# Values of all heads as seven products of quarters, with sums formed beside the state space

## The chip, the cores and the metric

The program runs on one core of one Trainium2 chip. The metric is the device time of one execution in microseconds. A profile of one execution gives, for every engine, what it did and what it waited for: TensorE (PE, with its weight loads as PEld), VectorE (DVE), ScalarE (ACT), GpSimd (POOL) and SyncE (SP). Here SP issues the program's DMAs, in one queue and in order.

## What is computed

A trunk of two layers over 1024 tokens of width 1024, in float32. Layer 0 projects the normalised input once and feeds a diagonal state space with a GLU beside a retention of 8 heads (4 pairs in the kernel). Layer 1 is a convolution module. The change concerns the retention's values `v` and the work in front of them.

```python
proj = h @ w_in                       # h = rmsnorm(x) * g, (1024, 1024)
u_s5, g_s5, q, k, v, g_ret = jnp.split(proj, cuts, axis=-1)   # v: (1024, 1024)
...
qc, kc = rope(q) * DK ** -0.5, rope(k)          # in chunks of 64 tokens
scores = jnp.einsum('bnihd,bnjhd->bnhij', qc, kc) * intra
intra_out = jnp.einsum('bnhij,bnjhe->bnihe', scores, vc)
kv = jnp.einsum('bnjhd,jh,bnjhe->bnhde', kc, k_dec, vc)
_, s_prev = lax.scan(state_step, zeros, kv)     # s <- chunk_decay * s + kv
cross = jnp.einsum('bnihd,ih,bnhde->bnihe', qc, q_dec, s_prev)
out = layernorm_per_head(intra_out + cross)
y_ret = out * jax.nn.silu(g_ret)
```

## The kernel before

**Matmuls.** Each float32 operand is split into a high part (cast to float32r) and a low part (the rest). A product is three matmuls: high x high, high x low, low x high. A matmul takes 128 rows of the inner dimension against 128 columns of the stationary and up to 512 of the moving operand; a full projection of one 128-column block and one half of the tokens (512) is 8 row blocks (`KB`) x 3.

**Scaling.** x is kept transposed (channels in partitions) and multiplied by the norm's gain `g`, but not by the reciprocal root of each token's mean square. This factor is applied when a result leaves PSUM: `R` along the free dimension for transposed results, `Rtok` per partition for results that have tokens in partitions, as the values do. `self.xs[h][kb]` holds the pair (high, low) of half h of the tokens and row block kb, in two rings of 16 buffers (`opA`, tags A0 and A1). They are held until the last projection has read them; then y, the state space's output, takes their place for the GLU.

**Weights.** `plan` lists all weight tiles (512 KB) in the order of their use. `wnext` issues the loads up to two tiles ahead; `wload` casts the high part on ScalarE and forms the low part on GpSimd or VectorE. There are three buffers of each kind.

**Order.** The program is built in an order of priorities, and the scheduler puts each engine's instructions into a fixed order with a model of the times. `issue_after(x)` keeps what it encloses behind the instruction x. `at(p)` sets a priority. On the chip every engine then keeps its own order and waits on semaphores. A pool's buffers are taken in rotation by tag; a pool that takes the place of a closed one waits for the old tiles.

**Stages.**

1. `layer0_front`: x is loaded and split; u projections (blocks 0 to 7); then 16 gate blocks (8 to 23), beside which the state space of 8 blocks runs: tables on GpSimd (`s5_tables`, one call per block, the last at gate block 19), the scan on VectorE (`s5_states`), outputs on TensorE (`s5_out`). At gate blocks 16 to 23 `weight_sums` forms sums of the output weights' quarters on VectorE and stores them: 4 loads, 4 operations and 4 stores of 256 KB for one half tile.
2. `retention`: for each of four pairs of heads `ret_proj` (k, then q, each 48 matmuls of 512 columns; evacuation on VectorE; the rotation by four DMAs that exchange rows, two products on GpSimd and an addition on VectorE), the values, two `y_pass` (gelu of two blocks of the state space's output, in pairs 1 to 3 behind the last rsqrt of the pair before), and `ret_heads`: transposed k (ktp), k-v products (kv) and their running state on VectorE, scores (sp), masked on VectorE, outputs (ro), the norm on VectorE and ScalarE, transposition back (rt) and the gate. There is one buffer each for the turned k and q, and two for their raw forms.
   - The values of pairs 0 and 1 come together in pair 0 (`ret_values_wide`): 2 token halves x 4 token blocks x 8 row blocks x 3 terms, 512 columns.
   - The values of pairs 2 and 3 come in those pairs (`ret_values`): 8 token blocks x 8 row blocks x 3 terms, 256 columns each.
   - Pair 2's k projection is asked for ahead of pair 1's heads (`ahead`).
   - In pair 0 `weight_low` forms 16 half tiles of low parts of the convolution's weights and stores them; the other 16 are formed in the GLU.
3. `layer0_back_and_layer1`: GLU, output projection (by seven products of quarters already), the convolution module, the last norm.

PSUM has 8 banks: 3 for projections (`mm`) and 5 for the rest (`aux`).

Of the kernel before, what the change touches and what calls it, by code (L numbers as in the profile page):

```python
# [11 lines left out]
F32 = mybir.dt.float32  # L12
# [7 lines left out]
P = 128  # L20
# [18 lines left out]
           [(i, nb) for i in (6, 7) for nb in range(4)] + [(4, nb) for nb in range(4)])  # L39


V_NG0, V_NG1, V_FG, V_GLUB, V_CB, V_LNG, V_LNB = range(7)


# [11 lines left out]
class Trunk:  # L56
# [22 lines left out]
    def plan(self):  # L79

        A = self.A
        seq = [(A["w_ab"][nb], f"u{nb}") for nb in range(8)]
        seq += [(A["w_ab"][nb], f"g{nb}") for nb in range(8, 24)]
        for p in range(4):
            seq += [(A["w_ab"][28 + p], f"k{p}"), (A["w_ab"][24 + p], f"q{p}")]

            if p == 0:
                seq += [(A["w_v"][j], f"v{p}_{h}_{j}") for h in range(2) for j in range(4)]
            elif p > 1:
                seq += [(A["w_v"][2 * p + i], f"v{p}_{i}") for i in range(2)]  # L90
# [17 lines left out]
        self.ws_d = {}  # L108
        self.wnames, self.lo_d = {n for _, n in seq}, {}

    def wnext(self, name, ahead=2):
# [8 lines left out]
    def wload(self, src, name):  # L120


        if src is None:
# [43 lines left out]
    def wload_sums(self, name):  # L167

        i, nb = int(name[1]), int(name[3])
        src = self.A["w_out"][{1: 0, 2: 8, 4: 12}[i] + nb] if i in (1, 2, 4) else self.ws_d[i, nb]  # L170
        return self.wload_split(self.wload_f32(src, name), name, self.nc.vector)

    def weight_low(self, pool, k, tags, bufs):

# [111 lines left out]
    def layer0_front(self, st):  # L286
# [134 lines left out]
        u_block(3)  # L421
        u_block(4)
        early.close()
        self.s5 = self.pool("s5w", 1, stack=st)
        sums = self.pool("sums", 1, stack=st)
        for nb in range(5, 8):
            u_block(nb)
        self.s5_tab, self.s5_back, self.s5_last = {}, {}, None
# [1 line left out]
        for nb in range(8, 24):  # L430
# [5 lines left out]
                self.s5_out(B - 1)  # L436
            if nb % 2 and B < 7:
                self.s5_tables(B + 1)
            if nb >= 16:
                with self.tc.issue_after(self.gate_evac.ins):  # L440
# [428 lines left out]

    def retention(self, st):  # L870
        nc, A = self.nc, self.A
        rp = self.rp = self.pool("ret", 1, stack=st)
        early = ExitStack()
        rq = self.rq = self.pool("retq", 1, stack=early, side="right")
        self.rk = rq.tile([P, 2, T], F32, name="ropek")
        nc.sync.dma_start(self.rk[:], A["rope_k"])
        self.mask = rp.tile([P, NH, P], F32, name="retmask")
        nc.sync.dma_start(self.mask[:], A["ret_mask"])
        self.kdec = rp.tile([P, NH, 64], F32, name="kdec")
        nc.sync.dma_start(self.kdec[:], A["ret_kdec"])  # L880
        self.g128 = rp.tile([P, 4], F32, name="g128")
        nc.sync.dma_start(self.g128[:], A["ret_g128"])
        self.reps = rp.tile([P, NH], F32, name="reteps")
        nc.sync.dma_start(self.reps[:], A["ret_eps"])
        ahead = None
        for pair in range(4):
            cur = list(ahead or self.ret_proj(pair))[-1]

            ahead = pair == 1 and self.ret_proj(pair + 1)
            if ahead:  # L890
                next(ahead)
            if pair == 0:
                V = self.ret_values_wide()
            elif pair > 1:
                V = self.ret_values(pair)
            with ExitStack() as held:
                if pair:
                    held.enter_context(self.tc.issue_after(self.last_rs.ins))
                for cb in (2 * pair, 2 * pair + 1):
                    self.y_pass(rq, cb)  # L900

            def turned():
                if pair == 3:
                    early.close()
                    self.lp = self.pool("l1", side="right")
            for k in range(LOWS if pair == 0 else 0):
                self.weight_low(rq, k, (("wa", "wb"), ("wc", "wd")), 2)
            self.ret_heads(pair, *cur, V, turned)

    def ret_proj(self, pair):  # L910
        nc, A, rp = self.nc, self.A, self.rp
        raws = {}

        def project(nm):
# [36 lines left out]
            qadds = ()  # L951
        yield krot, qrot, qadds

    def ret_values(self, pair):

        nc = self.nc
        wv = [self.wnext(f"v{pair}_{i}") for i in range(2)]
        vt = self.rp.tile([P, 8, 256], F32, name=f"v_{pair}", tag="v", bufs=2)
        for b in range(8):
            ps = self.bank(f"mm_v{pair}_{b}", aux=False)  # L960
            h, o = b // 4, (b % 4) * P
            for kb in range(KB):
                xh, xl = self.xs[h][kb]
                i, k4 = kb // 4, kb % 4
                wh = wv[i][0][:].rearrange("p (k a) n -> p k (a n)", a=2)[:, k4, :]
                wl = wv[i][1][:].rearrange("p (k a) n -> p k (a n)", a=2)[:, k4, :]
                nc.tensor.matmul(ps[:, :256], xh[:, o:o + P], wh, start=kb == 0, stop=False)
                nc.tensor.matmul(ps[:, :256], xh[:, o:o + P], wl, start=False, stop=False)
                nc.tensor.matmul(ps[:, :256], xl[:, o:o + P], wh, start=False, stop=kb == KB - 1)
            nc.scalar.mul(vt[:, b, :], ps[:, :256], self.Rtok[:, b:b + 1])  # L970
        return lambda p, b, hh: vt[:, b, hh * P:(hh + 1) * P]

    def ret_values_wide(self):

        nc = self.nc
        res = []
        for h in range(2):
            vt = self.rp.tile([P, 4, HALF], F32, name=f"v_0_{h}", tag="v", bufs=2)
            pss = [self.bank(f"mm_v0_{h}_{b}") for b in range(4)]
            for j in range(4):  # L980
                wh, wl = (t[:].rearrange("p (k a) n -> p k (a n)", a=4) for t in self.wnext(f"v0_{h}_{j}"))
                for b in range(4):
                    o = slice(b * P, (b + 1) * P)
                    for k in range(2):
                        kb = 2 * j + k
                        xh, xl = self.xs[h][kb]
                        nc.tensor.matmul(pss[b][:], xh[:, o], wh[:, k, :], start=kb == 0, stop=False)
                        nc.tensor.matmul(pss[b][:], xh[:, o], wl[:, k, :], start=False, stop=False)
                        nc.tensor.matmul(pss[b][:], xl[:, o], wh[:, k, :], start=False, stop=kb == KB - 1)
            for b in range(4):  # L990
                nc.scalar.mul(vt[:, b, :], pss[b][:], self.Rtok[:, 4 * h + b:4 * h + b + 1])
            res.append(vt)
        return lambda p, b, hh: res[b // 4][:, b % 4, (2 * p + hh) * P:(2 * p + hh + 1) * P]

    def ret_heads(self, pair, K, Q, qadds, V, turned):
        nc, rp = self.nc, self.rp
# [620 lines left out]
def layout(inp):  # L1617
# [10 lines left out]
    wv = w[:, 3072:4096].reshape(2, 4, P, 4, 256)  # L1628
    A["w_v"] = wv.transpose(3, 0, 2, 1, 4).reshape(8, P, KB, P)
    A["w_v"][:4] = w[:, 3072:3584].reshape(4, 2, P, HALF).transpose(0, 2, 1, 3).reshape(4, P, KB, P)  # L1630
# [49 lines left out]
```

## Time and profile before

| what | us |
|---|---|
| median of 3 runs | 1197.28 (1195.81 to 1198.75) |
| the profiled execution | 1195.29 |
| its span, first to last instruction | 1193.5 |
| TensorE busy | 1177.1 |
| VectorE, GpSimd, ScalarE busy | 870.5, 679.5, 533.8 |
| k and q of pair 0 on TensorE | 337.1 to 359.0 |
| values of pairs 0 and 1 | 359.0 to 402.5 |
| heads of pair 0, with k and q of pair 1 among them | 402.5 to 437.1 |
| heads of pair 1 begin, pair 2, pair 3 | 448.0, 494.6, 552.3 |

The mean granted clock of TensorE was 0.998 of full speed. How to read the views: a row of the stretches gives from:to in us, its length, then busy us and count for each engine, the granted clock, the mean busy share of the 16 DMA engines and GB/s. A row of the chain or of the timeline begins with start and duration. A row of a tile gives durations in ns (least/median/most) and the first and last start. "Busy" of pipelined matmuls says that some matmul was under way, not that the engine was at its peak.

### The profile page before, as it was taken

The page shows a single profiled execution, that of the slowest core. Times are in us where ns is not written, and L with a number is a line of the kernel's source. Part 1 is how long each engine was busy: PE and PEld are TensorE (multiplying, and loading weights), DVE is VectorE, ACT ScalarE, POOL GpSimd, SP SyncE. Part 2 cuts the span into 40 slices and gives each one's busy share as a digit, 9 for nine tenths or more (in the row PEclk, how much of TensorE's full clock was granted, in tenths as well). Part 3 has the DMA queues.
Part 4 walks back from the last instruction along what each step waited for, and adds up shares of the span by engine and source line. Part 5 has one row for each costly group of instructions (what it writes and reads, how often), then busy time and mean ns, then how long its engine had stood idle before and what let it go on. Part 6 is the DMA issues. An engine that isn't in the chain of part 4 may idle for free.

```text
span 1193.5 us, 17692 instructions
## 1 busy us (share of the span) xinstructions
PE 1177.1 (99%) x6390; PEld 987.1 (83%) x6390; DVE 870.5 (73%) x1455; ACT 533.8 (45%) x805; POOL 679.5 (57%) x481
## 2 busy tenths in 40 slices
PE   9999999999999999999899999999999999999997
PEld 7888888888888888989788888878887887888887
DVE  7875655699836358366876888379999999999643
ACT  7212233332334322235445535367756578444662
POOL 2059988888426345242443034338895678987642
PEclk9999999999999999999999999999999999999999
DMA  9353333388889463556897467866448653356873
GB/s 338 107 181 102 124 124 131 122 281 286 268 299 337 175 183 102 176 157 227 312 327 247 147 222 266 292 228 205 163 150 296 233 176 115 134 187 239 268 255 135
DMA packets 119097, 248.13 MB, mean 208 GB/s; under 512 B 11489, under 2 KB 40417, under 8 KB 118881
## 3 DMA queue, kind: packets, MB, share of 16 engines
q1 hardware_dynamic: 119008, 247.00, 61.0%
q8 instruction: 50, 0.82, 0.3%
q14 instruction: 39, 0.31, 0.1%
HBM read 179.39 MB, written 63.37 MB: 203 GB/s over the span
## 4 chain that ended last, share of the span: by engine, by line
PE 93%; DVE 3%; POOL 1%; DMA 1%; issue 1%; ACT 0%; SPq 0%; DVEq 0%; POOLq 0%; ACTq 0%
PE mm_g L227 7%; PE mm_g L226 7%; PE mm_g L225 7%; PE mm_w L225 4%; PE mm_w L226 4%; PE mm_w L227 4%; PE mm_oc L225 2%; PE mm_oc L226 2%; PE mm_oc L227 2%; PE mm_u L227 2%; PE mm_u L226 2%; PE mm_u L225 2%; PE mm_glu L227 2%; PE mm_glu L225 2%; PE mm_glu L226 2%; PE mm_b L226 2%
## 5 line engine op out<-in xcount | busy, mean ns | idle before, releaser
L1368 DVE SCALAR_TENSOR_TENSOR cv<-u,convw,cv 128x512 f32<-128x512 f32 x358 | 245.3, 749 | 5.7 <-ACT cv L1354 3.9
L1348 POOL TENSOR_TENSOR tp<-tp,tp 128x512 f32<-128x512 f32 x104 | 138.7, 1335 | 33.6 <-ACT tp L1347 27.8
L227 PE MATMUL mm_g<-xh,wl_g 128*128 128x512 f32 x256 | 100.8, 394 | 0.0
L226 PE MATMUL mm_g<-xl,wh_g 128*128 128x512 f32 x256 | 100.6, 393 | 0.0
L225 PE MATMUL mm_g<-xh,wh_g 128*128 128x512 f32 x256 | 100.4, 392 | 0.0
L1347 ACT ACTIVATE tp<-u,convw 128x512 f32<-128x512 f32 x104 | 69.3, 713 | 9.2 <-POOL tp L1348 9.0
L226 PEld LDWEIGHTS mm_g<-xl,wh_g 128*128 128x128 f32 x256 | 48.1, 188 | 11.3 <-issue 1.6
L227 PEld LDWEIGHTS mm_g<-xh,wl_g 128*128 128x128 f32 x256 | 48.1, 188 | 10.5
L225 PEld LDWEIGHTS mm_g<-xh,wh_g 128*128 128x128 f32 x256 | 48.1, 188 | 9.6
L225 PE MATMUL mm_oc<-zh,wh_woc 128*128 128x512 f32 (+1 forms) x152 | 54.5, 362 | 0.0
L227 PE MATMUL mm_oc<-zh,wl_woc 128*128 128x512 f32 (+1 forms) x152 | 54.5, 359 | 0.0
L226 PE MATMUL mm_oc<-zl,wh_woc 128*128 128x512 f32 (+1 forms) x152 | 54.2, 356 | 0.0
L1159 POOL TENSOR_TENSOR yg<-yg,yn 128x512 f32<-128x512 f32 x16 | 24.1, 1507 | 50.4 <-DMA yg<-gs_d 27.3
L226 PE MATMUL mm_u<-xl,wh_u 128*128 128x512 f32 x128 | 50.1, 391 | 1.0 <-DVE xl L339 0.9
L227 PE MATMUL mm_g<-h1h,wl_cg 128*128 128x512 f32 x128 | 50.0, 390 | 1.1 <-POOL wl_cg L217 1.1
L226 PE MATMUL mm_b<-h1l,wh_cb 128*128 128x512 f32 x128 | 50.5, 394 | 0.4 <-DVE h1l L1285 0.4
L225 PE MATMUL mm_glu<-yh,wh_glu 128*128 128x512 f32 x128 | 50.4, 394 | 0.0
L163 ACT CAST wh_p<-wf_p 128x1024 fp32r<-128x1024 f32 x28 | 29.5, 1053 | 46.7 <-PE mm_w L226 37.8
L225 PE MATMUL mm_g<-h1h,wh_cg 128*128 128x512 f32 x128 | 50.3, 393 | 0.0
L225 PE MATMUL mm_b<-h1h,wh_cb 128*128 128x512 f32 x128 | 49.9, 390 | 0.4 <-ACT h1h L1284 0.4
L227 PE MATMUL mm_a<-h1h,wl_ca 128*128 128x512 f32 x128 | 50.3, 393 | 0.0
L227 PE MATMUL mm_glu<-yh,wl_glu 128*128 128x512 f32 x128 | 50.2, 393 | 0.0
(790 smaller groups left out, 3664.8 us busy)
## 6 DMA issues: line engine op xcount, KB each, us to landing
wf_g<-w_ab SPq DMA_DIRECT2D x16, 512.0 KB, 5.2
a<-w_out SPq DMA_DIRECT2D x32, 256.0 KB, 5.3
ws<-a SPq DMA_DIRECT2D x32, 256.0 KB, 4.2
lf<-w_c SPq DMA_DIRECT2D x32, 256.0 KB, 5.7
wf_p<-ws SPq DMA_DIRECT2D x16, 512.0 KB, 3.8
wf_cb<-w_c SPq DMA_DIRECT2D x16, 512.0 KB, 4.7
wf_ca<-w_c SPq DMA_DIRECT2D x16, 512.0 KB, 4.8
wl_cb<-lo_cb SPq DMA_DIRECT2D x16, 512.0 KB, 3.4
```

Of the source, the lines that this page charges most:

```text
L163: self.nc.scalar.copy(wh[:].rearrange(fl), wf[:])
L225: nc.tensor.matmul(ps, wh[:, kb, :], xh, start=start, stop=False)
L226: nc.tensor.matmul(ps, wh[:, kb, :], xl, start=False, stop=False)
L227: self.last_mm = nc.tensor.matmul(ps, wl[:, kb, :], xh, start=False, stop=stop)
L1159: gp.tensor_tensor(yg[:], yg[:], yn[:], op=ALU.mult)
L1347: nc.scalar.mul(sk[:], u[:, k:k + HALF], cw[:, nb, k:k + 1])
L1348: gp.tensor_tensor(s0[:], s0[:], sk[:], op=ALU.add)
L1368: v.scalar_tensor_tensor(dst[:], *tap, accs_[i][:], op0=ALU.mult, op1=ALU.add)
```

## The change

The values of all four pairs are formed ahead of pair 0's heads. x (tokens x channels) and the weights of v (channels x columns) are cut into quarters of 512 x 512. Seven products of sums of quarters, each 512 x 512 x 512, replace the eight plain products; the four quarters of v are sums of the seven results, formed on VectorE as the products leave PSUM, and then scaled by `Rtok` on ScalarE.

- `input_sums` (new; at gate blocks 9, 11, 13, 15) forms four sums of x's quarters, times the gain, on ScalarE and VectorE and stores them in DRAM.
- `value_sums` (new; four half tiles at gate block 21, behind the last state-space table) forms four sums of the weights' quarters on GpSimd and stores them.
- `ret_values` (new form) runs the products in the order 1, 2, 6, 7, 3, 4, 5. Products 1, 2 and 3 use x's operands as they stand; for 6, 7, 4 and 5 `fetch` loads a stored sum of x and splits it into high and low part. Weights come as 14 tiles (`V1_0` to `V5_1`); products 6, 7, 3 and 5 take the stored sums.
- The values of pairs 2 and 3 are no longer formed in those pairs, and pair 2's k projection is no longer asked for ahead of pair 1's heads.
- `weight_low`'s 16 half tiles move from pair 0 to pairs 1 and 2, eight each, behind the masked scores of the pair before. `y_pass` of pair 0 and the load of `kdec` come after the values, since their pools are opened there. Pools are placed anew.

```diff
+V_ORDER = (1, 2, 6, 7, 3, 4, 5)
...
             if p == 0:
-                seq += [(A["w_v"][j], f"v{p}_{h}_{j}") for h in range(2) for j in range(4)]
-            elif p > 1:
-                seq += [(A["w_v"][2 * p + i], f"v{p}_{i}") for i in range(2)]
+                seq += [(None, f"V{i}_{j}") for i in V_ORDER for j in range(2)]
...
+    def wload_value(self, name):
+        i, j = int(name[1]), int(name[3])
+        src = self.A["w_v"][{1: 0, 2: 2, 4: 6}[i] + j] if i in (1, 2, 4) else self.vs_d[i, j]
+        return self.wload_split(self.wload_f32(src, name), name, self.nc.vector if i in (1, 2, 6) or j else self.nc.gpsimd)
+
+    def value_sums(self, pool, k):
+        j, c = k // 2, slice(k % 2 * HALF, (k % 2 + 1) * HALF)
+        e, a = self.nc.gpsimd, []
+        for q, (r, tag) in enumerate(((0, "wa"), (4, "wb"), (6, "wc"), (2, "wd"))):
+            a.append(pool.tile([P, HALF], F32, name=f"va{q}_{k}", tag=tag, bufs=2))
+            self.nc.sync.dma_start(a[q][:], self.A["w_v"][r + j].rearrange("p k n -> p (k n)")[:, c])
+        a11, s3, s2, s4 = (t[:] for t in a)
...
+        e.tensor_tensor(s3, a11, s3, op=ALU.subtract)
+        e.tensor_tensor(s2, s2, s3, op=ALU.subtract)
+        e.tensor_tensor(s4, s4, s2, op=ALU.subtract)
+        e.tensor_tensor(a11, a11, s2, op=ALU.add)
+        for i, t in ((7, s3), (6, s2), (3, s4), (5, a11)):
+            self.nc.sync.dma_start(self.vs_d[i, j][:, c], t)
+
+    def input_sums(self, pool, kb):
...
+        nc.scalar.mul(x11, x11, g1)
+        nc.scalar.mul(x12, x12, g1)
+        v.tensor_tensor(x11, x12, x11, op=ALU.subtract)
+        v.scalar_tensor_tensor(x12, x22, g2, x12, op0=ALU.mult, op1=ALU.subtract)
+        v.scalar_tensor_tensor(x22, x22, g2, x11, op0=ALU.mult, op1=ALU.subtract)
+        v.scalar_tensor_tensor(x21, x21, g2, x22, op0=ALU.mult, op1=ALU.subtract)
...
+            if nb == 21:
+                with self.tc.issue_after(self.s5_last.ins):
+                    for k in range(4):
+                        self.value_sums(sums, k)
+            with self.tc.issue_after(self.gate_evac.ins):
+                if nb >= 16:
                     self.weight_sums(sums, nb - 16)
+                elif nb % 2:
+                    self.input_sums(sums, (nb - 8) // 2)
...
         for pair in range(4):
-            cur = list(ahead or self.ret_proj(pair))[-1]
-            ahead = pair == 1 and self.ret_proj(pair + 1)
-            if ahead:
-                next(ahead)
+            cur = list(self.ret_proj(pair))[-1]
             if pair == 0:
-                V = self.ret_values_wide()
-            elif pair > 1:
-                V = self.ret_values(pair)
+                with ExitStack() as vst:
+                    V = self.ret_values(self.pool("vp", 1, stack=vst))
+                self.rp = self.pool("ret", 1, stack=st)
+                self.kdec = self.rp.tile([P, NH, 64], F32, name="kdec")
+                nc.sync.dma_start(self.kdec[:], A["ret_kdec"])
+                ry = self.pool("rety", 1, stack=early, side="right")
...
-            for k in range(LOWS if pair == 0 else 0):
-                self.weight_low(rq, k, (("wa", "wb"), ("wc", "wd")), 2)
+            if pair in (1, 2):
+                with self.tc.issue_after(self.masked[1].ins):
+                    for k in range(LOWS // 2 * (pair - 1), LOWS // 2 * pair):
+                        self.weight_low(ry, k, (("wa", "wb"), ("wc", "wd")), 1)
             self.ret_heads(pair, *cur, V, turned)
...
+        def fetch(i, slot):
+            res = []
+            for kb in range(4):
+                a, b = (vp.tile([P, HALF], F32R, name=f"xt{i}{q}{kb}", tag=f"xt{slot}", bufs=8) for q in "hl")
+                nc.sync.dma_start(b[:].bitcast(F32), self.xt_d[i][kb])
+                nc.scalar.copy(a[:], b[:].bitcast(F32))
+                v.tensor_tensor(b[:], b[:].bitcast(F32), a[:].bitcast(F32), op=ALU.subtract)
+                res.append((a, b))
+            return res
...
+        for n, i in enumerate(V_ORDER):
+            if i in (1, 2):
+                xs[i + 5] = fetch((2, 3)[i - 1], i)
+            pss = [self.bank(f"mm_v{i}_{b}", aux=n % 2 == 0 or b == 3) for b in range(4)]
+            for j in range(2):
+                wh, wl = (t[:].rearrange("p (k a) n -> p k (a n)", a=4) for t in self.wnext(f"V{i}_{j}"))
+                for b in range(4):
+                    o = slice(b * P, (b + 1) * P)
+                    for k in range(2):
+                        xh, xl = xs[i][2 * j + k]
...
+            if i in (6, 7):
+                xs[{6: 4, 7: 5}[i]] = fetch({6: 4, 7: 1}[i], i - 5)
+            for b, ps in enumerate(pss):
+                if i == 1:
+                    nc.scalar.copy(m[b][:], ps[:])
+                elif i in (2, 4):
+                    v.tensor_tensor(ps[:], ps[:], (m if i == 2 else u3)[b][:], op=ALU.add)
+                    scaled(i // 4, 0, b, ps[:])
+                else:
+                    v.tensor_tensor((u3 if i == 7 else m)[b][:], ps[:], m[b][:], op=ALU.add)
+                    if i == 5:
+                        scaled(0, 1, b, m[b][:])
+                        v.tensor_tensor(ps[:], ps[:], u3[b][:], op=ALU.add)
+                        scaled(1, 1, b, ps[:])
```

The layout of `w_v` on the host follows: eight tiles, two for each quarter of the weights.

More of the change, by code (lines that the diff above doesn't have):

```diff
@@ L107, in plan @@
         self.low_load, self.early_low = {}, None
-        self.ws_d = {}
+        self.ws_d, self.vs_d, self.xt_d = {}, {}, {}
         self.wnames, self.lo_d = {n for _, n in seq}, {}
@@ L120, in wload @@
     def wload(self, src, name):
+        if name[0] == "V":
+            return self.wload_value(name)
         if src is None:
@@ L171, in wload_sums @@
         return self.wload_split(self.wload_f32(src, name), name, self.nc.vector)
+    def wload_value(self, name):
[9 more added lines that the diff above has]
+        a11, s3, s2, s4 = (t[:] for t in a)
+        for i in (7, 6, 3, 5):
+            if (i, j) not in self.vs_d:
+                self.vs_d[i, j] = self.dram.tile([P, D], F32, name=f"vs{i}_{j}")
+        e.tensor_tensor(s3, a11, s3, op=ALU.subtract)
[4 more added lines that the diff above has]
+            self.nc.sync.dma_start(self.vs_d[i, j][:, c], t)
@@ new lines, in input_sums @@
+    def input_sums(self, pool, kb):
+        nc, v, a = self.nc, self.nc.vector, []
+        for q, tag in enumerate(("wa", "wb", "wc", "wd")):
+            a.append(pool.tile([P, HALF], F32, name=f"xa{q}_{kb}", tag=tag, bufs=2))
+            nc.sync.dma_start(a[q][:], self.A["xT"][kb + 4 * (q // 2), :, q % 2 * HALF:(q % 2 + 1) * HALF])
+        x11, x12, x21, x22 = (t[:] for t in a)
+        g1, g2 = self.vec(V_NG0, kb), self.vec(V_NG0, kb + 4)
+        nc.scalar.mul(x11, x11, g1)
[4 more added lines that the diff above has]
+        v.scalar_tensor_tensor(x21, x21, g2, x22, op0=ALU.mult, op1=ALU.subtract)
+        for i, t in ((2, x22), (3, x12), (4, x21), (1, x11)):
+            if i not in self.xt_d:
+                self.xt_d[i] = self.dram.tile([4, P, HALF], F32, name=f"xt{i}")
+            nc.sync.dma_start(self.xt_d[i][kb], t)
@@ L423, in layer0_front @@
         early.close()
+        sums = self.pool("sums", 1, stack=st)
         self.s5 = self.pool("s5w", 1, stack=st)
-        sums = self.pool("sums", 1, stack=st)
         for nb in range(5, 8):
@@ L871, in retention @@
         nc, A = self.nc, self.A
-        rp = self.rp = self.pool("ret", 1, stack=st)
+        r0 = self.r0 = self.pool("ret0", 1, stack=st)
         early = ExitStack()
         rq = self.rq = self.pool("retq", 1, stack=early, side="right")
+        self.vt = [[(r0 if d else rq).tile([P, 4, HALF], F32, name=f"v{d}_{h}") for h in range(2)] for d in range(2)]
         self.rk = rq.tile([P, 2, T], F32, name="ropek")
         nc.sync.dma_start(self.rk[:], A["rope_k"])
-        self.mask = rp.tile([P, NH, P], F32, name="retmask")
+        self.mask = r0.tile([P, NH, P], F32, name="retmask")
         nc.sync.dma_start(self.mask[:], A["ret_mask"])
-        self.kdec = rp.tile([P, NH, 64], F32, name="kdec")
-        nc.sync.dma_start(self.kdec[:], A["ret_kdec"])
-        self.g128 = rp.tile([P, 4], F32, name="g128")
+        self.g128 = r0.tile([P, 4], F32, name="g128")
         nc.sync.dma_start(self.g128[:], A["ret_g128"])
-        self.reps = rp.tile([P, NH], F32, name="reteps")
+        self.reps = r0.tile([P, NH], F32, name="reteps")
         nc.sync.dma_start(self.reps[:], A["ret_eps"])
-        ahead = None
         for pair in range(4):
-            cur = list(ahead or self.ret_proj(pair))[-1]
-            ahead = pair == 1 and self.ret_proj(pair + 1)
-            if ahead:
-                next(ahead)
+            cur = list(self.ret_proj(pair))[-1]
             if pair == 0:
-                V = self.ret_values_wide()
-            elif pair > 1:
-                V = self.ret_values(pair)
+                with ExitStack() as vst:
[4 more added lines that the diff above has]
+                ry = self.pool("rety", 1, stack=early, side="right")
             with ExitStack() as held:
@@ L899, in retention @@
                 for cb in (2 * pair, 2 * pair + 1):
-                    self.y_pass(rq, cb)
+                    self.y_pass(ry, cb)
             def turned():
@@ L952, in ret_proj @@
         yield krot, qrot, qadds
[L954 to L981, printed above, removed]
+    def ret_values(self, vp):
+        nc, v = self.nc, self.nc.vector
+        vt = self.vt
+        def fetch(i, slot):
[7 more added lines that the diff above has]
+            return res
+        def scaled(d, h, b, src):
+            nc.scalar.mul(vt[d][h][:, b, :], src, self.Rtok[:, 4 * h + b:4 * h + b + 1])
+        xs = {1: self.xs[0][:4], 2: self.xs[0][4:], 3: self.xs[1][4:]}
+        m, u3 = ([vp.tile([P, HALF], F32, name=f"{n}{b}") for b in range(4)] for n in ("vm", "vu"))
+        for n, i in enumerate(V_ORDER):
[4 more added lines that the diff above has]
+                wh, wl = (t[:].rearrange("p (k a) n -> p k (a n)", a=4) for t in self.wnext(f"V{i}_{j}"))
@@ L984, in ret_values_wide @@
                     for k in range(2):
-                        kb = 2 * j + k
-                        xh, xl = self.xs[h][kb]
-                        nc.tensor.matmul(pss[b][:], xh[:, o], wh[:, k, :], start=kb == 0, stop=False)
+                        xh, xl = xs[i][2 * j + k]
+                        first, last = j == k == 0, j == k == 1
+                        nc.tensor.matmul(pss[b][:], xh[:, o], wh[:, k, :], start=first, stop=False)
                         nc.tensor.matmul(pss[b][:], xh[:, o], wl[:, k, :], start=False, stop=False)
[L989 to L993, printed above, removed]
+                        nc.tensor.matmul(pss[b][:], xl[:, o], wh[:, k, :], start=False, stop=last)
+            if i in (6, 7):
[12 more added lines that the diff above has]
+                        scaled(1, 1, b, ps[:])
+        return lambda p, b, hh: vt[p // 2][b // 4][:, b % 4, (2 * (p % 2) + hh) * P:(2 * (p % 2) + hh + 1) * P]
     def ret_heads(self, pair, K, Q, qadds, V, turned):
@@ L1627, in layout @@
     A["w_ab"] = _blocks(order)
-    wv = w[:, 3072:4096].reshape(2, 4, P, 4, 256)
+    wv = w[:, 3072:4096].reshape(4, 2, P, 2, HALF)
     A["w_v"] = wv.transpose(3, 0, 2, 1, 4).reshape(8, P, KB, P)
-    A["w_v"][:4] = w[:, 3072:3584].reshape(4, 2, P, HALF).transpose(0, 2, 1, 3).reshape(4, P, KB, P)
     A["w_glu"] = _blocks(inp["s5_glu_w"][0][s5p][:, s5p])
```

4 lines of the change are left out of this document (1 added, 3 removed).

## The prediction

> **What bounds the kernel now.** I read the page first: who is busy, and who carries the chain that ended last.
>
> ```profile
> span 1193.5 us, 17692 instructions
> PE 1177.1 (99%) x6390; PEld 987.1 (83%) x6390; DVE 870.5 (73%) x1455; ACT 533.8 (45%) x805; POOL 679.5 (57%) x481
> PE 93%; DVE 3%; POOL 1%; DMA 1%; issue 1%; ACT 0%; SPq 0%; DVEq 0%; POOLq 0%; ACTq 0%
> ```
>
> TensorE is busy for 99% of the span and is 93% of the last chain. So a matmul taken away shortens the program, as long as other matmuls still cover what TensorE would otherwise wait for. The second view is the busy time by stretch, for the values' matmuls alone (mm_v). It gives their pitch, because the duration of one pipelined matmul is longer than the step to the next.
>
> ```profile
> core 0: us, PE busy (x) PEld busy (x) ACT busy (x), PEclk, DMA share, GB/s
> 358.90:402.50 43.60, 43.52 (x192) 35.91 (x192) 4.70 (x7) 1.00 0.96 322
> 529.20:552.25 23.05, 23.04 (x192) 22.98 (x191) 3.31 (x7) 1.00 0.67 223
> ```
>
> The values of pairs 0 and 1 are 192 matmuls of 512 columns: 43.52 / 192 = 0.2267 us each. Those of pair 3 are 192 of 256 columns at 0.1200 us, with the weight loads busy all the time. Pair 2's are the same 192 once more, interleaved with the heads of pair 1.
>
> The third view is busy time of all engines over the heads.
>
> ```profile
> core 0: us, PE busy (x) PEld busy (x) DVE busy (x) ACT busy (x) POOL busy (x), PEclk, DMA share, GB/s
> 402.50:437.10 34.60, 34.60 (x241) 29.32 (x240) 20.59 (x72) 10.40 (x11) 8.87 (x6) 1.00 0.33 98
> 552.25:590.80 38.55, 35.47 (x237) 30.15 (x236) 31.66 (x86) 18.16 (x27) 12.60 (x7) 0.96 0.81 294
> 552.50:576.00 23.50, 20.42 (x164) 17.55 (x163) 20.57 (x47) 9.71 (x16) 7.38 (x4) 0.94 0.86 309
> 576.00:600.00 24.00, 24.00 (x114) 19.94 (x114) 18.79 (x49) 12.40 (x17) 8.62 (x5) 0.98 0.81 287
> ```
>
> The first row is the heads of pair 0 with the k and q projections of pair 1 put between them. Those 96 matmuls of 512 columns are 96 x 0.2267 = 21.8 us, so the heads' own matmuls are 34.6 - 21.8 = 12.8 us. There is no gap. The second row is the heads of pair 3, beside which the GLU's matmuls stand: here 3.08 us are lost, and the clock falls. The waits of TensorE name the place:
>
> ```profile
> engine line waited for: us in total, times, longest us
> PE ro L1067 <- DVE sc L1046: 3.1, 1, 3.1
> ```
>
> By the last two rows such a stall costs more than itself: 23.5 us at clock 0.94 and 24.0 at 0.98 lose 1.4 + 0.5 = 1.9 us.
>
> **The change, part by part. Matmuls.** Removed: 192 of 512 columns, 43.5 us, and 384 of 256, 384 x 0.1200 = 46.1 us; together 89.6. Added: seven products of 4 token blocks x 4 row blocks x 3 terms = 336 of 512 columns, 336 x 0.2267 = 76.2 us. Difference -13.4 us, all on the chain of TensorE. About 11.2 of it is the eighth product that isn't formed; the rest is that 256 columns at 0.1200 us cost more than half of 0.2267.
>
> The Trainium skill, TensorE: Matmul & The Clock Gate, section Back-to-back issue gap, has N / 2.4 + 2.5 ns for a warm matmul. As an estimate that is 215.8 and 109.2 ns, 83.4 us before against 72.5 after, and a gain of 10.9 instead of 13.4; both measured pitches lie above it, and I go by the rows.
>
> **Sums beside the state space.** For x: four times 4 loads and 4 stores of 256 KB, 2 ScalarE products and 4 VectorE operations on 128x512. For the weights: four times 4 loads, 4 stores and 4 GpSimd operations. The nearest rows are the stage that already makes such sums for the output weights, at four VectorE operations per gate block, and the stretch behind the last table.
>
> ```profile
> 105.00:227.00 122.00, 122.00 (x828) 101.40 (x827) 67.66 (x94) 36.88 (x68) 102.41 (x79) 1.00 0.35 120
> 225.00:307.00 82.00, 82.00 (x540) 68.89 (x539) 76.33 (x85) 26.17 (x46) 74.01 (x53) 1.00 0.72 250
> 307.00:337.00 30.00, 30.00 (x232) 25.52 (x230) 21.82 (x29) 7.09 (x11) 7.85 (x4) 1.00 0.71 241
> ...
> 227.53 0.68 DVE L795 TENSOR_TENSOR v<-v,m 128x512 f32<-128x512 f32 x1
> 234.41 2.43 DVE L217 TENSOR_TENSOR wl_g<-wf_g,wh_g 128x1024 fp32r<-128x1024 f32 x1
> 236.76 1.90 DVE L199 TENSOR_TENSOR a<-a,a 128x512 f32<-128x512 f32 x1
> ...
> 305.46 1.62 POOL L726 TENSOR_TENSOR W<-W,o 128x512 f32<-128x512 f32 x1
> ```
>
> In the middle row VectorE is busy for 76.33 of 82 us, and TensorE loses nothing. The sums of x add 16 operations of 0.68 to 1.90 us, 11 to 30 us, to the first row's 67.66 of 122: at most 98 of 122, below the share of the middle row; ScalarE has 36.88 of 122, and 8 products more. The sums of the weights are 16 x 1.62 = 26 us of GpSimd once its last table ends at 307.1; with the 7.85 us it has there, they end near 341. Their first reader is the third product, near 359 + 2 x 10.9 = 381. I put both at nothing; if the 40 us of cover were gone, each us late would be a us of TensorE.
>
> The sums of the output weights share these buffers and wait in turn behind them. SP is one queue: a store that waits for GpSimd holds the loads behind it, namely the weights of q and of the first product, which TensorE takes near 348 and at 358.9. The 32 transfers are 8.4 MB in the last row's 30 us, which moves 241 GB/s already (7.2 MB); at the 322 GB/s of the values' first stretch, with the DMA engines at 0.96, both together need 48 us. But TensorE had no gap in that stretch, and the 8.4 MB of conv low parts leave it (below). Gain excluded, since nothing there leaves the path; loss 0 to 5 us. I take 0, because every such load goes out two weights ahead, some 11 us.
>
> A rule here speaks against the change: the Trainium skill, SBUF — State Buffer, section Who interferes with whom, says that a VectorE instruction with two SBUF inputs blocks against a GpSimd one that reads SBUF. The trace agrees, 1.90 us for the sum of two SBUF tiles against 0.68 for the state-space step, whose first operand is in PSUM; by it the state-space chain isn't slowed.
>
> **Beside the seven products.** ScalarE and VectorE take what TensorE must not wait for.
>
> ```profile
> L991 ACT ACTIVATE v<-mm_v,Rtok x8: 682/686/691, 379.9 to 402.7; 128x512 f32<-128x512 f32 x8
> L181 ACT CAST lh<-lf x32: 603/621/627, 353.4 to 631.7; 128x512 fp32r<-128x512 f32 x32
> L182 DVE TENSOR_TENSOR lh<-lf,lh x32: 669/692/2845, 354.0 to 632.7; 128x512 fp32r<-128x512 f32 x32
> ...
> L163 ACT CAST wh_p<-wf_p 128x1024 fp32r<-128x1024 f32 x28 | 29.5, 1053 | 46.7 <-PE mm_w L226 37.8
> ...
> wf_v<-w_v SPq DMA_DIRECT2D x12, 512.0 KB, 5.7
> ```
>
> VectorE: 28 additions out of PSUM at 0.69 = 19 us, 16 low parts of x sums at 0.69 = 11, 10 low parts of weights at up to 2.43 = 24; 54 of 76 us. ScalarE: 20 evacuations at 0.69 and 16 casts at 0.62 are 24 us, and 14 weight casts at 1.05 are 15 more; 39 of 76. Weights: 14 loads in 76.2 us, one every 5.4, as before (8 in 43.5), landing in 5.7 and asked for two ahead. Banks: a product takes four, and the next but one takes them again 10.9 us later. Cost nothing; at the end the last bank needs an addition and a product where it needed one product, 0.7 us later, ahead of the first heads' 5 us of other matmuls.
>
> **What leaves the heads.** This is the other half of the change, and its price. The matmuls of pair 2's and 3's values stood between heads; now k and q alone are left, and the early k of pair 2 isn't asked for ahead any more. The chain in order of time, and the way from the last q to its turned form:
>
> ```profile
> 337.18 0.43 PE mm_k L225
> ...
> 402.67 0.44 PE ktp L1004 x4
> 410.04 1.31 PE sp L1040 x18
> 432.97 0.87 PE rt L1095 x8
> 552.41 0.45 PE ktp L1004 x4
> ...
> 529.41 0.69 DVE L921 TENSOR_TENSOR qraw<-mm_q,R 128x512 f32<-128x512 f32 x1 [2.56 <-PE mm_q L227]
> 554.09 1.64 DVE L937 TENSOR_TENSOR qrot<-qrot,qswp 128x512 f32<-128x512 f32 x2
> ...
> 539.27 3.34 POOL L936 TENSOR_TENSOR qswp<-qswp,ropek 128x512 f32<-128x512 f32 x2 [3.87 <-DMA qswp<-qraw]
> ```
>
> q of pair 3 leaves TensorE at 529.2. Its exchanged rows have landed at 539.3, GpSimd ends at 542.6, and the addition takes 1.6: the scores (sp) can begin 15.0 us behind the last q. From sp to the last transposition (rt) is 410.04 to 433.84, 23.8 us. So from the last q to the end of its heads are 38.8 us, with 12.8 of own matmuls: 26.0 have to be covered. The next pair's k and q give 21.8, and 4.2 are missing. Before, 23 us of values covered that for pairs 2 and 3, and the early k for pair 1.
>
> For pairs 1 and 2 the missing 4.2 can be taken from k of the pair after: two raw buffers let it run before its turn. For pair 3 there is no such k, and the GLU needs x's operand buffers, which are free only behind the last q projection, and all of the gelu's rows. I take 4.2 + 1.9 of clock = 6.1 us there, and nothing for the others; the bounds are 0 and three times 6.1 = 18.3.
>
> The 16 low parts of the conv weights (per piece one load and one store of 256 KB, 0.62 of ScalarE, 0.69 of VectorE) move from beside the values to the heads of pairs 0 to 2, eight in each of two turns. VectorE there: 20.6 of the row, one more evacuation 0.7, four additions of turned k and q at 0.7 to 1.8, and 8 x 0.69 = 5.5, so 30 to 34 of 34.6 us. It fits with nothing to spare. The gelu of pair 0's two blocks (two loads and two stores of 512 KB) and the load of kdec move behind the values on SP. The gelu's reader is the GLU, 100 us on. kdec's is the first operation behind ktp, but its place comes free with the sixth product, one product (10.9 us) ahead, for a load that lands in some 6. Both at nothing.
>
> Sum: -13.4 + 6.1 = -7.3 us. The profiled execution took 1195.29 (span 1193.5), so 1188.0; its median run is 1197.28, by which it is 1190.0, and I give that one. What a measurement can tell from no change is 0.3%, 3.6 us.
>
> **The rivals.** *The cover holds everywhere.* The order of TensorE fills pair 3's gap with GLU matmuls on the first six row blocks. For it: only the last two gelu blocks are late. -13.4, 1183.9.
>
> *The cover is missing at every pair.* VectorE at 30 to 34 of 34.6 us delays the heads, and k of the pair after isn't ready to be put in, since its raw buffer or its weights are late. Three times 6.1 gives -13.4 + 18.3 = +4.9, 1202.2, slower. It decides from 13.4 / 3 = 4.5 us lost per pair. For it: the stall of 3.1 us in the heads of pair 3, where such low parts stand already and VectorE has 31.66 of 38.55. Against it: no gap in pair 0's heads, and VectorE only at 20.59.
>
> *Two pairs pay.* -13.4 + 12.2 = -1.2, 1196.1, no difference to be told.
>
> *The sums are late or hold SP*, so that the change doesn't give seven dense products: the 13.4 go in waits ahead of the third product; about 1200, slower.
>
> **How the numbers follow.** Forecast 0.38, cover everywhere 0.23, missing at every pair 0.20, two pairs 0.13, sums late 0.06. Faster 0.61, same 0.13, slower 0.26. The forecast's own range is 1187 to 1193. The range of 8 in 10 takes in the full cover with 2 us for the old stall that may shrink, 1181.9, and the lighter half of the slower cases, up to 1202.5; so 1182 to 1202.5.
>
> **What would show it.** Right: 336 matmuls of mm_v in about 76 us with no wait; the first heads' transposition (ktp) near 435; pair 3's ktp near 539 against 552.4; one wait of TensorE on sc or a turned q in pair 3, with a clock dip behind it. Wrong: waits of TensorE before sp of pairs 1 and 2, a wait on wl_V or xt inside the products, or k of pair 0 starting later than 337.

## The result, and the profile after

The changed kernel took 1212.63 us (median of 4 runs, 1208.0 to 1214.84) against 1198.01 for the kernel before: ratio 1.0112, interval 1.0068 to 1.0156. It is slower, where 1190 was forecast. The profiled execution took 1213.96. Its page, then the waits of TensorE:

```profile
span 1212.2 us, 17495 instructions
PE 1173.8 (97%) x6150; PEld 972.0 (80%) x6150; DVE 920.3 (76%) x1525; ACT 550.4 (45%) x827; POOL 681.7 (56%) x489
PE 77%; DMA 8%; DVE 7%; POOL 2%; issue 2%; ACT 2%; SPq 1%; DVEq 0%; POOLq 0%; ACTq 0%
```

```profile
PE y L896 <- ACT W L881: 7.8, 1, 7.8
PE sp L1098 <- DVE qrot L986: 6.4, 3, 3.8
PE kv L1081 <- DVE kt L1064: 2.9, 1, 2.9
PE ktp L1062 <- DVE krot L986: 2.7, 2, 1.6
PE ro L1125 <- DVE sc L1104: 1.4, 1, 1.4
```

TensorE carries 77% of the last chain instead of 93%, and it waits in two places: ahead of the retention, for block 7 of the state space, and among the heads. Busy time by stretch (from:to, length, PE, PEld, DVE, ACT, POOL, clock, DMA share, GB/s):

```profile
337.00:347.80 10.80, 6.12 (x49) 5.77 (x49) 4.17 (x6) 4.21 (x6) 0.71 (x1) 0.57 0.99 326
369.70:447.30 77.60, 77.60 (x337) 63.13 (x336) 45.51 (x55) 34.17 (x47) 25.67 (x14) 1.00 0.52 161
447.30:569.50 122.20, 112.76 (x740) 94.72 (x739) 92.11 (x252) 49.53 (x59) 45.29 (x28) 0.96 0.73 235
569.50:611.90 42.40, 37.38 (x240) 30.48 (x239) 32.93 (x87) 20.12 (x29) 13.39 (x8) 0.96 0.88 330
```

| mark on TensorE | before | forecast's sum | after |
|---|---|---|---|
| k of pair 0 begins | 337.1 | 337.1 | 347.8 |
| seven products (values of pairs 0, 1 before) | 359.0 to 402.5 | 76.2 long | 369.7 to 447.3 |
| first to fourth pair's heads | 402.5 to 552.3 | 103.7 long | 447.3 to 569.5 |
| end of pair 3's heads | 590.8 | 583.5 | 611.9 |

So 10.7 us are lost in front, 1.4 in the products (their matmuls on fetched sums of x step by 0.234 us instead of 0.227; no run shows why), and most of the rest in the 122.2 us between the first transpositions of pair 0 and pair 3. That stretch holds k, q and heads of three pairs, 103.8 us by the prediction's prices (3 x 34.6), and 18 GLU matmuls pulled ahead, 4.1. So 14.3 us are lost: 9.4 in which TensorE stood, 4.9 by the clock (0.04 of 122.2).

**In front.** The timeline of SP before; after; then ScalarE's after:

```profile
319.46 0.33 SPq L826 DMA_DIRECT2D k_d<-Kt  x1
321.00 0.38 SPq L829 DMA_DIRECT2D Wd<-k_d  x1
```

```profile
327.06 0.38 SPq L196 DMA_DIRECT2D vs<-va  x1
327.53 3.02 SPq L876 DMA_DIRECT2D k_d<-Kt  x1
331.08 0.90 SPq L196 DMA_DIRECT2D vs<-va  x2
333.62 0.98 SPq L879 DMA_DIRECT2D Wd<-k_d  x1
```

```profile
319.63 0.26 ACT L874 COPY Kt<-kt 128x128 f32<-128x128 f32 x1
340.59 1.04 ACT L881 COPY W<-Wd 128x1024 f32<-128x1024 f32 x1 [16.86 <-DMA Wd<-k_d]
```

Block 7's small tile Kt is ready at 319.9. Its store stands in SP's order behind the weight sums' transfers and goes out at 327.5; the load of Wd follows at 333.6, and `s5_out` starts with it at 341.7. Before the change the two transfers went out at 319.5 and 321.0.

**Among the heads.** The chain that ended last, at the scores of pair 1 and a little later:

```profile
478.92 2.09 ACT yn L917
481.40 4.81 DMA yp<-y_d
486.31 2.05 ACT yn L917
488.81 0.56 SPq L915
489.45 0.82 SPq L979
491.61 5.34 DMA qswp<-qraw
497.10 1.27 POOL qswp L985
498.40 1.75 DVE qrot L986
500.28 2.47 PE sp L1098 x18
...
512.21 5.08 DMA lf<-w_c
517.37 0.63 ACT lh L225
518.02 0.69 DVE lh L226
519.04 0.48 DVE st L1139 x2
```

Two things stand on the way. The exchange of q's rows (L979) is issued behind the gelu's transfers, which wait for ScalarE. And VectorE, in its fixed order, has a low part (lh) of a convolution weight ahead of the statistics (st) of the heads; that low part waits for its load.

### The profile page after: what moved, and what is told of

It is laid out like the page before. It is cut to its first block, busy times and chain, and to the rows that moved or that the text cites. A ratio compares the mean times of both kernels' runs of the same rounds, so it can differ in the third digit from the quotient of the medians.

```text
span 1212.2 us, 17495 instructions
## 1 busy us (share of the span) xinstructions
PE 1173.8 (97%) x6150; PEld 972.0 (80%) x6150; DVE 920.3 (76%) x1525; ACT 550.4 (45%) x827; POOL 681.7 (56%) x489
## 4 chain that ended last, share of the span: by engine, by line
PE 77%; DMA 8%; DVE 7%; POOL 2%; issue 2%; ACT 2%; SPq 1%; DVEq 0%; POOLq 0%; ACTq 0%
PE mm_g L271 6%; PE mm_g L270 6%; PE mm_g L269 6%; PE mm_w L269 4%; PE mm_w L270 4%; PE mm_w L271 3%; PE mm_u L271 2%; PE mm_u L270 2%; PE mm_oc L271 2%; PE mm_oc L269 2%; PE mm_oc L270 2%; PE mm_u L269 2%; PE mm_v L1036 2%; PE mm_v L1034 2%; PE mm_v L1035 2%
## 5 line engine op out<-in xcount | busy, mean ns | idle before, releaser
L270 PEld LDWEIGHTS mm_g<-xl,wh_g 128*128 128x128 f32 x256 | 48.1, 188 | 11.3 <-issue 1.6
L270 PE MATMUL mm_glu<-yl,wh_glu 128*128 128x512 f32 x128 | 50.5, 395 | 0.2 <-DVE yl L1165 0.2
L269 PE MATMUL mm_u<-xh,wh_u 128*128 128x512 f32 x128 | 49.4, 396 | 1.2 <-ACT wh_u L260 1.1
```

What stands on the lines that cost most here:

```text
L269: nc.tensor.matmul(ps, wh[:, kb, :], xh, start=start, stop=False)
L270: nc.tensor.matmul(ps, wh[:, kb, :], xl, start=False, stop=False)
```

## The experiments

The question was which of four things costs what: the place of the weight sums, the gelu's transfers, the low parts, or the cover that the values' matmuls had given. Every ratio below is against the kernel before on the same chip; the heads' stretch always runs from pair 0's first transposition to pair 3's.

**1. The weight sums later.**

```diff
-            if nb == 21:
-                with self.tc.issue_after(self.s5_last.ins): ... value_sums
+        with self.tc.issue_after(self.s5_wd.ins):   # block 7's load of Wd
+            for k in range(4):
+                self.value_sums(sums, k)
         self.s5_out(7)
```

> The changed kernel with the weight sums' loads held behind block 7's load of its convolution tile (Wd) instead of behind the last table. Theory (SP's queue: the sums' stores and loads stand ahead of block 7's two small transfers): the 7.8 us wait of the state space's last output goes, k of pair 0 begins near 337 instead of 347.8, and the program takes about 1202, 10 to 11 us less. Rival (the sums are simply too much work there): the wait moves to the third product, and the time stays within 3 us of 1212.

1220.43 us, ratio 1.0169 (1.0145 to 1.0194): slower still. The wait of `y` is gone and k begins at 336.6, but a wait as long stands at the third product. Waits of TensorE, the stretch, and SP:

```profile
PE mm_v L1033 <- ACT xt2h L1012: 13.1, 1, 13.1
```

```profile
382.00:395.00 13.00, 0.13 (x1) 0.14 (x1) 6.45 (x8) 5.80 (x10) 5.58 (x3) 0.58 0.80 274
```

```profile
377.36 7.16 SPq L196 DMA_DIRECT2D vs<-va  x3
```

SP holds x's sums behind stores that wait for GpSimd's last weight sums. The rival was right that the wait moves to the third product; its time, within 3 us of 1212, was missed as the theory's was. The sums now stood too late.

**2. The low parts back beside the values** (in the buffers of the raw and exchanged k and q).

```diff
+                    for k in range(LOWS):
+                        self.weight_low(rq, k, None, 2)   # tiles "swp", "raw"
...
-            if pair in (1, 2):  ... weight_low
```

> The changed kernel with the 16 low parts of the convolution's weights back beside the values (in the buffers of the raw and exchanged k and q, which are free there), the rest as it is. Theory (the low parts hold SP, ScalarE and VectorE in the heads): from pair 0's first transposition to pair 3's takes 105 to 110 us instead of 122.2, waits on the turned q shrink, and the program takes 1196 to 1202. Rival (the cover is missing whatever else stands there, 4.2 us and 1.9 of clock a pair): the stretch stays at 116 to 122 and the program at 1207 to 1212.

1214.68 us, 1.0136 (1.0115 to 1.0157). Stretch and waits within it:

```profile
448.60:571.10 122.50, 112.47 (x740) 95.08 (x739) 78.32 (x237) 41.08 (x44) 43.08 (x28) 0.94 0.54 169
```

```profile
PE sp L1100 <- DVE qrot L988: 10.0, 2, 5.6
```

The stretch is no shorter. With the low parts gone all that TensorE stands is at the turned q. At the longer of the two waits the chain runs through a gelu: SP issues its store at 527.6, and only then, from 528.5, the exchange of q's rows.

**3. Both** edits of 1 and 2 in one kernel.

> Both of the above. If both theories hold the parts add: 1185 to 1192, below the kernel before. If the cover is missing: about 1198 to 1202.

1226.07 us, 1.0232 (1.0217 to 1.0247): the third product waits 19.4 us for x's sums, and the stretch is 122.0. Neither part helped in the place that I gave it.

**4. The kernel before without the values of pairs 2 and 3.**

```diff
-            elif pair > 1:
-                V = self.ret_values(pair)
```

> The kernel before without the values of pairs 2 and 3 (part of the computation is left out: those pairs read the values of pairs 0 and 1), so that the cover goes and nothing else comes. It keeps the early k of pair 2. If the cover costs nothing for want of other matmuls: 46.1 us less, about 1151. By the 6.1 us a pair of the prediction's slower case, for pairs 2 and 3 only: about 1163; more if y's transfers are late as well.

1164.32 us in one run, 33.9 below the 1198.22 of the kernel before on the same chip. So 12.2 of the 46.1 us come back. By the mean that is the 6.1 a pair of the slower rival, but the trace doesn't show it pair by pair. Two stretches, then a wait of TensorE and pieces of the chain ahead of it:

```profile
402.20:479.40 77.20, 77.20 (x517) 65.24 (x516) 50.01 (x151) 19.40 (x22) 31.12 (x19) 1.00 0.43 128
479.40:522.90 43.50, 35.55 (x225) 30.38 (x224) 30.68 (x82) 13.19 (x16) 14.34 (x9) 0.88 0.50 144
```

```profile
PE ro L1063 <- DVE sc L1042: 4.6, 1, 4.6
494.13 6.71 DMA yf<-yn_d
502.41 1.74 DVE yl L1103
504.16 1.20 DVE sc L1042 x2
```

Pairs 0 and 1 lose nothing. Pair 2's stretch holds 12.8 us of its own matmuls and 79 of 512 columns (k, q and GLU), 17.9 us, so 12.8 of its 43.5 us are lost; in pair 3 TensorE stands for 2.4 us, where it stood for 3.1. In pair 2 VectorE has a low part of the GLU's operand (yl) ahead of the masked scores (sc), and yl waits for its load. So the agreement with 6.1 a pair is luck: one pair pays all of it, and its longest wait comes from VectorE's order.

**5. The weight sums earlier, on VectorE.**

```diff
                 elif nb % 2:
                     self.input_sums(sums, (nb - 8) // 2)
+                else:
+                    self.value_sums(sums, (nb - 8) // 2)   # e = nc.vector
```

> The changed kernel with the weight sums at gate blocks 8, 10, 12 and 14, on VectorE instead of GpSimd, the rest as it is. Theory (their place, not their amount, costs the front 10.7 us and the later place cost 13.1 us at the third product): no wait of the state space's last output, none at the third product, k of pair 0 near 337, the products 359 to 436, and about 1202. Rival (what the sums take is lost wherever they stand, here as VectorE's time in the state space): k begins 5 us late or more, 1207 or above.

1207.08 us, 1.0072 (1.0054 to 1.009), 5.5 less than the changed kernel by the medians and 9.8 less by the profiled spans. No wait of `y` or of the third product; k begins at 338.4. So the place of the sums cost the front 9.4 of its 10.7 us; the engine changed with the place, and no run parts the two. The stretch of the heads is 122.0 as before. The time expected, 1202, was missed by 5: it is the rival's time with the theory's marks, and the profiled execution, 1204.21, is the fastest of the four.

**6. The gelu passes beside the values.**

```diff
+                    for cb in range(8):
+                        self.y_pass(rq, cb)        # tiles "swp", "raw"
...
-                for cb in (2 * pair, 2 * pair + 1):
-                    self.y_pass(ry, cb)
```

> The changed kernel with all eight gelu passes beside the values (in the buffers of the raw and exchanged k and q) and none in the heads, the rest as it is. Theory (the exchange of q's rows is issued late because a gelu's store, which waits for ScalarE, stands ahead of it on SP): q's rows land 5 us earlier for pairs 1 and 2, the waits on the turned q go from 6.4 us to under 2, and the program takes 1203 to 1208. Rival (cover alone: 15 us from q to its scores with 21.8 us of matmuls whatever is on SP): the waits stay within 2 us of 6.4 in sum, 1210 to 1214.

1208.03 us, 1.0074 (1.005 to 1.0097). The waits on the turned q are gone, as expected, but the stretch is 120.8, of which 1.6 are seven more GLU matmuls: other waits have come in their place.

**7. Experiments 5 and 6 together.**

> Both. If both hold: 1192 to 1198, at or below the kernel before. If only the place of the sums counts: about 1202.

1201.65 us, 1.003 (1.0009 to 1.0051): 0.3% slower than before. Stretch and waits in it:

```profile
440.30:560.70 120.40, 112.29 (x747) 93.42 (x746) 94.73 (x255) 32.70 (x55) 46.55 (x29) 0.99 0.60 190
```

```profile
PE ktp L1056 <- DVE krot L980: 5.9, 4, 3.0
PE rt L1147 <- DVE on L1139: 1.8, 1, 1.8
```

What is late now is VectorE's own work, behind the low parts. The chain ahead of the longest of these waits:

```profile
517.88 0.63 ACT lh L225
518.53 0.69 DVE lh L226
519.83 4.29 DVE krot L980 x2
```

The two additions of the turned k take 4.3 us there, and 2.4 in experiment 8.

**8. The same, with all 32 low parts in the GLU.**

```diff
-LOWS = 16
+LOWS = 0
```

> Both, and all 32 low parts of the convolution's weights in the GLU, none in the heads. Theory (with SP free of the gelu, the low parts are what is left on VectorE and SP in the heads): the stretch from pair 0's first transposition to pair 3's goes to 105 to 110 us, and if the GLU covers 32 as it covers 16, 1186 to 1192, faster than the kernel before. Rival (they cost nothing in the heads, as putting them beside the values showed): same as the run before, or 2 to 5 us slower by the GLU's load.

1222.67 us, 1.0201 (1.018 to 1.0222). The heads did what the theory said, and the GLU did not. The stretch; the longest wait of the program; and the chain ahead of it:

```profile
439.00:547.90 108.90, 108.67 (x743) 91.95 (x742) 78.49 (x239) 21.58 (x37) 44.73 (x28) 1.00 0.43 132
```

```profile
PE mm_w L269 <- ACT m L1285: 27.2, 1, 27.2
```

```profile
674.12 3.81 DMA lf<-w_c
678.03 0.63 ACT lh L225
678.68 0.70 DVE lh L226
679.82 3.76 DMA lf<-w_c
```

In the stretch TensorE stands for 0.2 of 108.9 us, at full clock, with the same 720 matmuls of k, q and heads as in all the others, and 22 of the GLU (18 in the changed kernel, 25 in 6 and 7): no cover is missing. The 27.2 us are the low parts' chain in the GLU: their buffers are also the places of the output projection's first sums.

**9 to 11. Three pairs of buffers for the low parts in the GLU; then 8, then 4 of the 32 left in the heads (pair 1's turn).**

```diff
-                self.weight_low(lp, k, (("cs", "pilot"), ("cq", "sq")), 1)
+                self.weight_low(lp, k, (("cs", "pilot"), ("cq", "sq"), ("lxa", "lxb")), 1)
```

> As the run before (sums early, gelu beside the values, all 32 low parts in the GLU), with a third pair of buffers for the low parts in the GLU. Theory (the 27.2 us wait ahead of the output projection is the chain load, cast, subtraction, store of two buffer pairs, and the heads lose nothing): the wait shrinks by a third of the chain or more, to under 8 us, the heads stay at 109 us, and the program takes 1190 to 1200; without any wait there 1189 to 1192, faster than the kernel before. Rival (the GLU has no room for 32): the wait stays above 15 us and the program above 1207.

1207.91 us, 1.0073 (1.0057 to 1.0089). The stretch stays at 109.0; the wait ahead of the output projection falls to 13.0, not to under 8, and the time is the rival's (above 1207).

```diff
-LOWS = 0
+LOWS = 8                   # experiment 11: 4
...
+            if pair == 1:
+                with self.tc.issue_after(self.masked[1].ins):
+                    for k in range(LOWS):
+                        self.weight_low(ry, k, (("wa", "wb"), ("wc", "wd")), 1)
```

> The same with 8 of the 32 low parts in the heads (pair 1's turn) and 24 in the GLU with three pairs of buffers. Theory: the GLU's chain fits, no wait ahead of the output projection; 8 low parts among the heads cost about half of what 16 do (5 to 6 us of the 11.4 by which the stretch grew), so 1193 to 1198. Rival (a low part among the heads costs only where it meets a pair without the values; pair 2 is then free): the stretch near 111 us and 1188 to 1192.

1194.57 us (12 runs, 1188.3 to 1201.97), 0.9971 (0.9951 to 0.9991): faster than both kernels, than the one before by 0.3%, and within what was expected. No wait is left ahead of the output projection.

```profile
443.40:558.50 115.10, 111.58 (x746) 93.51 (x745) 87.42 (x247) 27.81 (x47) 45.88 (x28) 0.99 0.52 162
```

> The run before with 4 low parts in the heads and 28 in the GLU. If a low part among the heads costs 0.75 us each (8 cost 6.2, 16 cost 11.5), the stretch of the heads is 112 us instead of 115.1; if the GLU's chain is the limit, which waited 13.0 us with 32 and not at all with 24, the wait ahead of the output projection is 0 to 6 us. Together 1190 to 1198: under 1194 if the GLU still has room, 1195 to 1198 if it has not.

1196.89 us (12 runs, 1191.48 to 1201.83), 0.998 (0.9962 to 0.9999). In the profiled execution four low parts among the heads cost nothing to be seen, not 3 us, and what is left is the wait ahead of the output projection. But that execution is the fastest of the 12, 5.4 us below their median, while experiment 10's profile (1197.47) lies above its own; which of the two places is better these runs don't tell.

```profile
439.50:548.90 109.40, 109.40 (x747) 92.57 (x745) 84.94 (x243) 25.77 (x43) 45.13 (x28) 1.00 0.49 151
```

```profile
PE mm_w L269 <- ACT m L1285: 3.3, 1, 3.3
```

## Why the prediction was wrong

The heads' stretch by what stands in it besides the matmuls:

| | low parts in the heads | low parts elsewhere |
|---|---|---|
| gelu in the heads | 122.2 (after), 122.0 (5) | 122.5 (2), 122.0 (3) |
| gelu beside the values | 120.8 (6), 120.4 (7) | 108.9 (8), 109.0 (9) |

The first row holds 18 GLU matmuls as well, 6 and 7 hold 25, 8 and 9 hold 22. Less these, at 0.2267 us each, and less 103.8, the loss is 14.1 to 14.6 us in the first row, 11.3 and 10.9 in 6 and 7, and 0.1 and 0.2 in 8 and 9. "Elsewhere" is beside the values in 2 and 3 and in the GLU in 8 and 9; no run has the low parts in the GLU with the gelu in the heads.

- **Matmuls, -13.4.** Right: 336 matmuls in 77.6 instead of 76.2 us, with no wait in the products. VectorE was busy for 45.5 us beside them (54 was the bound), ScalarE for 34.2 (39). The saving is 12.0.
- **The sums beside the state space, "both at nothing".** Wrong, by 10.7 us, twice the bound of 5. The step that failed is the list of what is held on SP: it named weight loads, which go out two ahead, and left out block 7's own two transfers, which go out when they are ready and have no lead. The queue was in the prediction; not everything in it was. The rival that has the sums hold SP got a chance of 0.06, and looked for the wait at the third product. Experiments 1 and 5 show that the place did it: later, the third product waits; earlier, and on VectorE, neither place does.
- **"Nothing for the others" among the pairs.** Wrong as a time, right as a count of matmuls. 14.3 us were lost where 0 was forecast for pairs 1 and 2. But k of the pair after does run ahead, and in experiment 8 it covers everything. The slower rival's price, 18.3 for three pairs, was near, but its reason, that cover is missing because k of the pair after isn't ready, falls with experiment 8. Its other reason, VectorE delaying the heads, was partly right: by order, not by busy time. That experiment 4 met its 6.1 a pair is luck.
- **The low parts and the gelu, "at nothing".** This is the step that failed among the heads. The prediction put the low parts at nothing by VectorE's busy time, priced of the gelu only pair 0's two blocks, and left out the passes of pairs 1 to 3, which stay in the heads. Either one alone in the heads loses 10.9 to 14.6 us; with neither the loss is 0.2 at most, and with both it is no more than with the gelu alone: the chain of a pair is late by SP or by VectorE's order, and it is late once. Busy shares did not show it: VectorE is busy for 92 of 122 us after, and for 78 of 109 where nothing is lost. I had counted its busy time (30 to 34 of 34.6 us a pair) and not what its fixed order waits for.
- **Pair 3, 6.1.** The GLU's matmuls did run ahead there, 18 to 25 of them. Pair 3's heads take 42.4 us instead of 38.6, with three GLU matmuls more, so 3.2 are added; with the 10.7 and the 14.3, less the 12.0 saved, that is 16.2 of the 18.7 us between the two profiles, and the rest lies behind the heads. A wait on masked scores stays: 3.1 us before, 1.4 in the changed kernel, 2.7 to 4.3 in experiments 7 to 11. The 15.0 us from q to its scores were read from a place where nothing was urgent: the way takes 12.3 to 13.5 us in pairs 1 to 3 of experiment 8, and 19.1, 17.3 and 14.4 in the changed kernel.
- **Still open.** With the sums early, k begins at 337.9 to 340.3 instead of 337.1. In experiment 10 (340.2) TensorE stands for 1.5 us between 105 and 227 us, where it had no gap before; the rest was not followed, nor why its runs spread over 13.7 us. Whether its gain grows with a better place for the last low parts wasn't settled either.

## What to carry to other kernels

Matmuls that look like surplus can be the time in which a single DMA queue works off its backlog; before taking them away, list for each step everything that its queue and its engines have in front of it, above all transfers that nobody issues ahead. Put side work where nothing serial waits behind it: the same sums cost 10.7 us, a wait of 13.1 us, or one to three, by place (the early ones ran on VectorE as well). A stretch can lose 14.3 of 122.2 us to order while every engine beside TensorE is busy for less than 80% of it.

## What the hardware showed besides

A wait of some us costs clock as well. In the stretch 337.0 to 347.8, which holds the last 4.7 us of the wait of 7.8, the mean granted clock is 0.57, and in 382 to 395 of experiment 1, nearly all of it a wait, it is 0.58; over the heads' 122.2 us the dips cost 4.9 us beside 9.4 of standing. The Trainium skill, TensorE: Matmul & The Clock Gate, section Part 1: The HAM clock gate, says that after an idle window of about 3.4 us the clock is halved. The traces agree with the half: in the changed kernel the granted clock is 0.50 from 534.04 to 537.46. They show too that shorter waits can bring it about: just ahead TensorE waits for 1.6 us at 531.0 and 1.1 at 533.3, and from 530.60 to 534.04 it is busy for 1.03 of 3.44 us.
